# A hybrid encoder layer on one core: which early block stores the split weights, and where the last columns' raw weights are split

## The chip, the core and the metric

The kernel runs on one core of one Trainium2 chip. The metric is the device time of one execution in microseconds (us); smaller is better. The profile is of one other execution of the same program. Its engines are named PE (matmul) and PEld (its weight loads), DVE (VectorE), ACT (ScalarE), POOL (GpSimd) and SP (SyncE, which here only issues DMA).

## The reference

One layer of a streaming encoder over 2048 prompt rows, 16 meta rows and 64 sample rows of width 1024, all in float32. Cut to what matters here:

```python
def _trunk(x, states, segs, p):
    ...
        m, ns = _mixer(_rmsnorm(x, p['norm1_w'][l]), l, *st, segs, p)
        x = x + m
        x = x + _swiglu(_rmsnorm(x, p['norm2_w'][l]), p['w_gate'][l], p['w_up'][l], p['w_down'][l])
    ...
    return _rmsnorm(x, p['final_norm_w']), [jnp.stack(lst) for lst in new]

def _swiglu(h, wg, wu, wd):
    return (jax.nn.silu(h @ wg) * (h @ wu)) @ wd
```

`_mixer` is one input projection, three parallel groups of recurrent heads (SSD, RWKV-7, HGRN2) and one output projection of their 1536 outputs. `w_gate` and `w_up` are 1024 x 2816, `w_down` is 2816 x 1024. The outputs are the normed rows and the heads' states.

## The kernel before

**Numbers in two parts.** Each float32 matmul is made of three products of parts: a high part (`hi`, a copy on ACT into the float32r type) and a low part (`lo`, the difference from the raw number). `load_unit` (L191 to L206) brings one unit of weights, 128 x 512 numbers, into the ring: a tile `w` with both parts (512 KB, 5 buffers, WB) and, when the unit has not been split yet, a tile `raw` (256 KB, 3 buffers, RB). The first time, it loads `raw` (L200, on SP), copies to `hi` (L201, ACT), subtracts for `lo` (L203: three units of four on POOL, the fourth on DVE) and stores both parts in DRAM (L205, on SP); the dictionary `split` remembers where. Each later time it loads both parts in one DMA (L197).

**Stages.** The 17 row tiles are first projected in three double chunks (`projection`, from 0 to about 1350 us in the profile). Two streams of mixers are woven into everything up to about 2600 us: `flow` adds up the cost that each piece of the main stream yields and steps a mixer when its due time has come. The first nine tiles then go through `Ffn` in three early blocks of three tiles (320, 384 and 384 rows, `EARLY`); in order: the output projection `out`, with 24 units of `w_out`, and `ffn` over the 22 columns f of the hidden layer. For every f, `gemm_cm` (L238) takes two units of `w_gate` (k0 = 0 and k0 = 4) and two of `w_up`, with 12 matmuls each, and yields 12 x rows/2360 us of cost for each. Columns go in pairs (CF = 2); for a pair `down_units` loads four units of `w_down` (two columns by two halves of the output), and `down_tile` adds their products to `acc`, a yield of 3 x 2 x 512/2360 for each tile and half. That is 132 units for each block. So block 1 (`fs[0]`) splits and stores all of them, and blocks 2 and 3 load parts. For block 2 the pieces of the FFN yield 11 x (8 x 1.95 + 6 x 1.30) = 258 units of cost in all.

**Sums of quarters.** The last eight tiles take another path (`tokens_first` and `columns`) that needs sums of weight quarters. After the output projection of block 2, `prep_sums` is added as a stream: twelve groups, 35 cost units apart, of four raw loads (`t_sums`, L1367, on SP, into the same three `raw` buffers), four subtractions or additions on DVE (L1375 to L1383) and four stores (L1372, on POOL's queue).

**The end of block 3.** Block 3 runs `ffn(0, SWITCH)` with SWITCH = 18 beside the mixers. When these are done, the columns from 18 on and `rest` run as `last_early`, woven with `last_rows`, which loads the 24 pieces of mixer output that the last eight tiles need (`ya`, L1494), each with rows in pieces of 512 bytes; both take SP's queue.

**The last norm.** At the end of `tokens_first("wd", ...)`, `final_norm` (L1147) takes each of four chunks: squares of the second half on ACT (L1145; those of the first half were taken earlier, after product a12, in `rows_done`), their sum on DVE (L1154), the inverse root on POOL (L211), two multiplications of 128 x 512 on DVE (L1158), and two stores.

The order of each engine's instructions is set at build time by a scheduler with a timeline of its own. A piece may so be issued far ahead of its place in the program, as soon as a buffer is free; among pieces that want the same kind of buffer the program's order holds.

## Time and profile before

| what | us |
|---|---|
| three timed runs: median (lowest, highest) | 3490.52 (3483.44, 3492.62) |
| the profiled execution, its own time | 3493.2 |
| its span, first to last instruction | 3491.4 |
| early block 1, FFN (132 units) | 1452 to 1863 |
| early block 2, FFN | 1905 to 2310 |
| early block 3, FFN up to column 18 | 2352 to 2600 |
| early block 3, the last columns | 2600 to 2710 |
| the last eight tiles | 2710 to the end |

The page gives the span and the engines' busy time. Below them stands each resource in 40 slices of 87 us: the digit is its busy share in tenths, and the last row gives what the 16 DMA engines moved.

```profile
span 3491.4 us, 61048 instructions
...
DMA  8776875665776667999899897786778568875866
GB/s 312 230 235 213 291 229 169 178 176 162 230 236 190 195 191 263 313 321 317 310 315 320 314 330 245 241 270 217 230 244 260 199 206 276 299 266 169 292 191 215
```

The eight slices of 310 to 330 GB/s from the 17th on are blocks 1 and 2. In rows of the views by line, the form is: line, engine, operation, tiles written and read, shape, count, then busy time, mean ns of one, and idle time before it with what ended it. In rows of one line's instructions it is: count, shortest/median/longest ns, first and last start in us. A stage's row gives its length, each engine's busy time with its count of instructions, the granted PE clock, the busy share of the DMA engines, and GB/s.

### The profile page before, as it was taken

Reading aid. Unit: us, or ns where it says so; the run is one execution under the profiler, and the core shown is the slowest. Engines: PE = TensorE matmul, PEld = TensorE weight load, DVE = VectorE, ACT = ScalarE, POOL = GpSimd, SP = SyncE. Lnnn points to the kernel's source line nnn. Section 1 sums busy time; section 2 is a strip of 40 time slices with the busy share of each in tenths; the row PEclk is TensorE's granted clock in tenths of the full one; section 3 lists DMA queues with packets and bytes.
Section 4 is the critical chain, followed back from the end, with each engine's and each line's share of the span. In section 5 each row is a group of like instructions: output and inputs, shape, how many; then the busy total and the mean of one; then the engine's idle time right before and its main releaser. Section 6 shows DMA issues by size and latency. Waiting matters only on the chain.

```text
span 3491.4 us, 61048 instructions
## 1 busy us (share of the span) xinstructions
PE 3357.3 (96%) x22588; PEld 2936.8 (84%) x22588; DVE 2206.7 (63%) x4978; ACT 1238.9 (35%) x2678; POOL 783.0 (22%) x1122
## 2 busy tenths in 40 slices
PE   7999999999999999898998999999999999999998
PEld 7999689999789997787777888979888887888787
DVE  4268565477766676777877567676643675665453
ACT  4445333344443343453452212242211352233342
POOL 3324202102112112444442111011100123431001
PEclk9999999999999999999999999999999999999999
DMA  8776875665776667999899897786778568875866
GB/s 312 230 235 213 291 229 169 178 176 162 230 236 190 195 191 263 313 321 317 310 315 320 314 330 245 241 270 217 230 244 260 199 206 276 299 266 169 292 191 215
DMA packets 427123, 860.42 MB, mean 246 GB/s; under 512 B 112432, under 2 KB 212280, under 8 KB 424776
## 3 DMA queue, kind: packets, MB, share of 16 engines
q1 hardware_dynamic: 394376, 749.01, 65.5%
q0 software_dynamic: 32448, 107.50, 8.4%
q8 instruction: 178, 2.92, 0.3%
q14 instruction: 121, 0.99, 0.1%
HBM read 603.81 MB, written 252.54 MB: 245 GB/s over the span
## 4 chain that ended last, share of the span: by engine, by line
PE 69%; DMA 11%; DVE 10%; issue 4%; ACT 2%; POOL 2%; SPq 2%; POOLq 0%; DVEq 0%; ACTq 0%
PE g L109 47%; PE d L109 11%; PE c L109 5%; PE h L109 4%; DMA w<-w 3%; DMA raw<-in_w_up 1%; DMA raw<-in_w_out 1%; DVE gcv L407 1%; POOL w L203 1%; DVE Xp L630 1%; DVE tp L629 1%; PE po L109 1%; DMA hg<-stage 1%; DMA b4k<-psc 1%; DMA raw<-in_w_gate 1%
## 5 line engine op out<-in xcount | busy, mean ns | idle before, releaser
L109 PE MATMUL g<-hhi,w 128*128 128x384 f32 (+3 forms) x5424 | 1388.7, 333 | 27.8 <-DMA w<-w 10.8
L109 PEld LDWEIGHTS g<-hhi,w 128*128 128x128 f32 x5424 | 961.3, 190 | 53.4 <-DMA w<-w 10.4
L109 PE MATMUL g<-hlo,w 128*128 128x384 f32 (+3 forms) x2736 | 901.6, 330 | 1.3 <-DVE hlo L236 1.2
L109 PEld LDWEIGHTS g<-hlo,w 128*128 128x128 f32 x2736 | 516.4, 189 | 10.9 <-DVE hlo L236 2.2
L203 POOL TENSOR_TENSOR w<-raw,w 128x512 fp32r<-128x512 f32 x180 | 249.9, 1390 | 328.3 <-ACT w L201 262.8
L109 PE MATMUL g<-w,hhi 128*128 128x512 f32 (+1 forms) x832 | 273.3, 407 | 17.5 <-DMA w<-w 14.1
L109 PE MATMUL g<-w,mhi 128*128 128x512 f32 x792 | 263.3, 407 | 9.6 <-ACT w L201 3.8
L201 ACT ACTIVATE w<-raw 128x512 fp32r<-128x512 f32 x240 | 150.1, 627 | 178.0 <-PE g L109 51.5
L109 PEld LDWEIGHTS g<-w,hhi 128*128 128x128 f32 (+1 forms) x832 | 152.5, 189 | 55.4 <-DMA w<-w 16.6
L109 PEld LDWEIGHTS g<-w,mhi 128*128 128x128 f32 x792 | 146.6, 189 | 45.9 <-DVE acc L1323 6.5
L629 DVE TENSOR_TENSOR tp<-Xp,b4k 128x60 f32<-128x60 f32 (+24 forms) x527 | 122.0, 231 | 71.2 <-DMA b4k<-psc 58.4
L109 PE MATMUL g<-w,hlo 128*128 128x512 f32 (+1 forms) x416 | 165.9, 401 | 0.0
L109 PE MATMUL g<-w,mlo 128*128 128x512 f32 x396 | 158.0, 399 | 0.0
L1323 DVE TENSOR_TENSOR acc<-g,acc 128x512 f32<-128x512 f32 (+1 forms) x198 | 133.1, 682 | 34.1 <-PE g L109 34.0
L109 PE MATMUL g<-w,op 128*128 128x512 f32 x600 | 142.8, 396 | 0.0
L109 PEld LDWEIGHTS g<-w,op 128*128 128x128 f32 x600 | 112.6, 188 | 27.1
L630 DVE TENSOR_TENSOR Xp<-Xp,tp 128x60 f32<-128x60 f32 (+24 forms) x527 | 124.5, 236 | 13.1
L345 DVE SCALAR_TENSOR_TENSOR stage<-graw,cvec,stage 128x384 f32<-128x384 f32 (+2 forms) x98 | 55.1, 564 | 117.6 <-ACT graw L340 50.9
L109 PE MATMUL d<-ya,w 128*128 128x512 f32 x528 | 124.4, 392 | 0.7 <-DMA w<-w 0.7
L211 POOL TENSOR_TENSOR rs<-ss,half 128x1 f32<-128x1 f32 (+2 forms) x51 | 36.4, 719 | 378.7 <-DVE ss L209 236.2
L109 PEld LDWEIGHTS d<-ya,w 128*128 128x128 f32 x528 | 99.1, 188 | 22.8 <-DMA w<-w 1.1
L109 PE MATMUL d<-w,op 128*128 128x512 f32 x492 | 115.9, 396 | 0.0
(455 smaller groups left out, 5941.0 us busy)
## 6 DMA issues: line engine op xcount, KB each, us to landing
w<-w SPq DMA_DIRECT2D x893, 512.0 KB, 4.3
hin<-hg SPq DMA_DIRECT2D x16, 1280.0 KB, 7.1
rin<-rw SPq DMA_DIRECT2D x16, 896.0 KB, 5.7
raw<-in_w_gate SPq DMA_DIRECT2D x56, 256.0 KB, 4.6
raw<-in_w_up SPq DMA_DIRECT2D x56, 256.0 KB, 5.1
hg<-stage SPq DMA_DIRECT2D x64, 192.0 KB, 2.5
raw<-in_w_out SPq DMA_DIRECT2D x48, 256.0 KB, 5.3
sin<-ss SPq DMA_DIRECT2D x16, 768.0 KB, 4.9
```

What stands on the lines that cost most here:

```text
L109: return T.matmul(out, lhsT, rhs, start=start, stop=stop, skip_group_check=more)
L201: S.activation(hi, raw, AF.Copy)
L203: (G if units[0] % 4 < GLO else V).tensor_tensor(lo, raw, wt[:, 0], SUB)
L211: G.tensor_tensor(rs[:n], ss[:n], half[:n, 0:w], ALU.pow)
L345: V.scalar_tensor_tensor(st[:, a0:a1], raw[:, s0:s0 + a1 - a0], mu, st[:, a0:a1], MUL, ADD)
L407: V.scalar_tensor_tensor(cvt[:, :M], raw[:, j:j + M], tap(j), cvt[:, :M], MUL, ADD)
L629: V.tensor_tensor(tv, _bc(Xp[:, 0:m, q], 2, w), _bc(Up[:, q, q + 1:32], 1, m), MUL)
L630: V.tensor_tensor(Xp[:, 0:m, q + 1:32], Xp[:, 0:m, q + 1:32], tv, ADD)
L1323: V.tensor_tensor(self.acc[:n, i, cs], ps[:n], self.acc[:n, i, cs], ADD)
```

## The change

Four edits in one:

- `load_unit` takes `keep` and `again`. Without `keep`, a raw unit is split and not stored, so the next block that wants it loads it raw once more. With `again`, a unit is loaded raw and split although its parts are in DRAM.
- `Ffn.keep(k0)`: in block 1, only the units with k0 = 0 (for `w_down`, the first column of a pair) are stored. Block 2 loads the parts of these, and loads raw, splits and stores the others. `w_out` goes as before. `Ffn.again(f)`: in block 3, the 24 units of the columns from 18 on are loaded raw and split, and not stored.
- `last_rows` issues the 24 loads of `ya` from POOL's queue instead of SP's, ordered by row half, chunk and group rather than by group first, with one yield for each instead of two.
- `final_norm`, where the first half's squares were taken ahead (the last four chunks): that half is multiplied by the norm's weight on DVE right after its squares, in `rows_done`, and at the end by the inverse root alone, on ACT; the second half stays on DVE.

```diff
@@ -188,12 +188,13 @@
     units = [0]
     split = {}
 
-    def load_unit(src):
+    def load_unit(src, keep=True, again=False):
+
 
         key = str(src)
         wt = mk(ring, [P, 2, 512], F32, tag="w", bufs=WB)
         hi, lo = wt[:, 0].bitcast(F32R), wt[:, 1].bitcast(F32R)
-        if key in split:
+        if key in split and not again:
             nc.sync.dma_start(wt, split[key])
             return hi, lo
         raw = mk(ring, [P, 512], tag="raw", bufs=RB)
@@ -201,6 +202,8 @@
         S.activation(hi, raw, AF.Copy)
         units[0] += 1
         (G if units[0] % 4 < GLO else V).tensor_tensor(lo, raw, wt[:, 0], SUB)
+        if again or not keep:
+            return hi, lo
         d = split[key] = dram.tile([P, 2, 512], F32, tag=f"w{units[0]}", name=f"w{units[0]}")
         nc.sync.dma_start(d, wt)
         return hi, lo
@@ -235,11 +238,11 @@
         S.activation(ho, pt[:, :, :n], AF.Copy)
         V.tensor_tensor(lw, pt[:, :, :n], ho.bitcast(F32), SUB)
 
-    def gemm_cm(w, hTs):
+    def gemm_cm(w, hTs, keep=lambda k0: True, again=False):
 
         banks = [gbank() for _ in hTs]
         for k0 in range(0, KD, 4):
-            hi, lo = load_unit(w[:, k0 * P:(k0 + 4) * P])
+            hi, lo = load_unit(w[:, k0 * P:(k0 + 4) * P], keep(k0), again)
             for ps, ((hhi, hlo), n) in zip(banks, hTs):
                 for k in range(k0, k0 + 4):
                     wh, wl = (x[:, (k - k0) * P:(k - k0 + 1) * P] for x in (hi, lo))
@@ -1146,6 +1149,8 @@
 
     def final_norm(p, xt, t, n, fw, queue, s2=None):
 
+
+        weighted = s2 is not None
         ss = mk(p, [P, 1], tag="ss", bufs=2)
         if s2 is None:
             s2 = mk(p, [P, 2], tag="s2", bufs=2)
@@ -1155,7 +1160,10 @@
         rs = inv_rms(p, ss, n, 1, 1.0 / D, EPS)
         for hf in range(2):
             cs = slice(hf * 512, hf * 512 + 512)
-            V.scalar_tensor_tensor(xt[:, cs], xt[:, cs], rs[:n], fw[:n, cs], MUL, MUL)
+            if weighted and hf == 0:
+                S.activation(xt[:, cs], xt[:, cs], AF.Copy, scale=rs[:n])
+            else:
+                V.scalar_tensor_tensor(xt[:, cs], xt[:, cs], rs[:n], fw[:n, cs], MUL, MUL)
             queue.dma_start(O["y_prompt"][(t - 1) * P:t * P, cs] if t else O["y_sample"][:, cs], xt[:, cs])
 
     class Ffn:
@@ -1278,8 +1286,8 @@
             for f0 in range(fa, fb, CF):
                 mhi, mlo = self.hl(self.fp, "m", CF, 2)
                 for f in range(f0, f0 + CF):
-                    pg, = yield from gemm_cm(A["w_gate"][f], [(self.hT, self.N)])
-                    pu, = yield from gemm_cm(A["w_up"][f], [(self.hT, self.N)])
+                    pg, = yield from gemm_cm(A["w_gate"][f], [(self.hT, self.N)], self.keep, self.again(f))
+                    pu, = yield from gemm_cm(A["w_up"][f], [(self.hT, self.N)], self.keep, self.again(f))
                     sg = self.w2k()
                     h_, l_ = mhi[:, f - f0, NS], mlo[:, f - f0, NS]
                     S.activation(sg[:, NS], pg[:, NS], AF.Tanh, scale=0.5)
@@ -1310,7 +1318,16 @@
                     yield 3 * CF * 512 * COL
 
         def down_units(self, f0, hf):
-            return [load_unit(A["w_down"][f * P:(f + 1) * P, hf * 512:hf * 512 + 512]) for f in range(f0, f0 + CF)]
+            return [load_unit(A["w_down"][f * P:(f + 1) * P, hf * 512:hf * 512 + 512], self.keep(4 * (f - f0)), self.again(f))
+                    for f in range(f0, f0 + CF)]
+
+        def keep(self, k0):
+
+            return k0 == 0 or self is not fs[0]
+
+        def again(self, f):
+
+            return self is fs[-1] and f >= SWITCH
 
         def down_tile(self, i, hf, mhi, mlo, wds):
             o, n, cs = self.offs[i], self.lens[i], slice(hf * 512, hf * 512 + 512)
@@ -1488,11 +1505,10 @@
     ya = {m: mk(lqa, [P, 2, 4, 512], F32, tag="ya", bufs=3) for m in (2, 0, 1)}
 
     def last_rows():
-        for m in (2, 0, 1):
-            for h in range(2):
-                for j in range(NH):
-                    nc.sync.dma_start(ya[m][:, h, :, j * P:j * P + P], yscr[m][tile_of(h, j)])
-                    yield 0.0
+        for h in range(2):
+            for j in range(NH):
+                for m in (2, 0, 1):
+                    G.dma_start(ya[m][:, h, :, j * P:j * P + P], yscr[m][tile_of(h, j)])
                     yield 0.0
 
     def last_early():
@@ -1733,6 +1749,7 @@
                 final_norm(l2, acc[1][j], tile_of(1, j), P, fw, G)
             elif a == "a12":
                 squares(l2, acc[0][j], P, 0, sq[j])
+                V.tensor_tensor(acc[0][j][:, :512], acc[0][j][:, :512], fw[:, :512], MUL)
 
     acc = [[mk(l2, [P, D], tag=f"acc{h}{j}", bufs=1) for j in range(NH)] for h in range(2)]
     fw = mk(l2, [P, D], tag="nw", bufs=1)
```

## The prediction

> **What bounds the kernel now.** I began with the page: which engine is busy, and how large a load of weights is.
>
> ```profile
> PE 3357.3 (96%) x22588; PEld 2936.8 (84%) x22588; DVE 2206.7 (63%) x4978; ACT 1238.9 (35%) x2678; POOL 783.0 (22%) x1122
> ...
> w<-w SPq DMA_DIRECT2D x893, 512.0 KB, 4.3
> ```
>
> PE is busy 96% of the span, so only a stage in which PE lacks something can give time back. PE's busy time hides short gaps, because matmuls overlap; weight loads (PEld) show them better. So next I read the busy time by stage: the projection, the FFN of early block 1, that of block 2, the FFN of block 3 while the mixers run, and its end in two pieces.
>
> ```profile
> core 0: us, PE busy (x) PEld busy (x) DVE busy (x) ACT busy (x) POOL busy (x), PEclk, DMA share, GB/s
> 60.00:350.00 290.00, 284.59 (x1931) 272.88 (x1929) 155.46 (x366) 133.56 (x288) 105.25 (x168) 0.99 0.72 231
> ...
> 1452.00:1863.00 411.00, 383.49 (x3003) 331.14 (x3003) 321.49 (x669) 173.86 (x376) 180.84 (x148) 0.97 0.91 318
> ...
> 1905.00:2310.00 405.00, 396.34 (x2904) 350.94 (x2906) 275.59 (x663) 105.84 (x253) 67.81 (x89) 0.99 0.82 280
> ...
> 2352.00:2600.00 248.00, 243.70 (x1888) 222.48 (x1886) 146.37 (x357) 53.84 (x131) 25.22 (x27) 0.99 0.71 226
> 2600.00:2640.00 40.00, 29.57 (x121) 26.43 (x120) 19.85 (x23) 6.15 (x8) 0.00 (x0) 0.83 1.04 315
> 2640.00:2710.00 70.00, 70.00 (x353) 63.21 (x352) 25.47 (x43) 8.00 (x19) 1.16 (x3) 1.00 0.71 234
> ```
>
> PEld's share is 331.14/411 = 0.81 in block 1, 350.94/405 = 0.87 in block 2, 222.48/248 = 0.90 in block 3, and 0.66 against 0.90 in the last two rows. So block 1 and the 40 us at 2600 are the loose places. Block 1 is also where DMA is busiest over a long time (0.91 of the engines, 318 GB/s), since it reads raw weights and writes both parts back. What ends last there is seen in the chain of work within that window, and in its raw loads (L200), copies (L201) and subtractions (L203):
>
> ```profile
> by line: PE g L109 30.3%; DMA raw<-in_w_up 8.1%; PE c L109 5.9%; issue 5.3%; POOL w L203 5.1%; DMA raw<-in_w_down 5.0%; PE h L109 3.7%; DMA raw<-in_w_gate 3.4%; DMA hin<-hg 1.9%; DVE acc L1323 1.8%; DMA w<-w 1.7%; ACT w L201 1.6%; DVE Xp L6
> ```
> ```profile
> DMA to landing us min/median/max: 3.2/4.7/9.3
> ```
> ```profile
> L201 ACT ACTIVATE w<-raw x127: 612/631/682, 1459.0 to 1821.2; 128x512 fp32r<-128x512 f32 x127
> ```
> ```profile
> L203 POOL TENSOR_TENSOR w<-raw,w x96: 1262/1298/2667, 1452.0 to 1823.6; 128x512 fp32r<-128x512 f32 x96
> ...
> L203 DVE TENSOR_TENSOR w<-raw,w x33: 655/684/1698, 1451.6 to 1820.7; 128x512 fp32r<-128x512 f32 x33
> ```
>
> The second of these fences is the landing of the raw loads (min, median, max). Block 1's FFN has 132 units (22 columns f with 4 gate and up units and 2 down units each). The copies of 127 of them lie 362.2/126 = 2.87 us apart. With three raw buffers one trip of a buffer takes 3 x 2.87 = 8.6 us: 4.7 landing, 0.63 copy, 1.14 subtraction (three of four on POOL), and 2.1 of issue and waits. So block 1 runs partly at the pace of the raw ring, and loads are 8.1 + 5.0 + 3.4 = 16.5% of its chain, 68 us.
>
> **Part 1: fewer stores in block 1.** Units with k0 = 4 and the second down unit of each pair are no longer stored: 66 of 132, 66 x 0.524 = 34.6 MB and 66 issues on SP fewer. Block 1 now moves 411 us x 318 GB/s = 131 MB; 96 MB remain, 251 GB/s at 383 us. The projection, at 231 GB/s, shows what a raw load (L200) takes when DMA has room:
>
> ```profile
> DMA to landing us min/median/max: 3.2/3.8/5.0
> ```
>
> By line between 3.8 at 231 and 4.7 at 318 GB/s, loads land in 4.0, which is 0.7 sooner; a trip takes 7.9 us, a unit 2.64, and 132 units gain 30 us. Two bounds: if only loads on the chain count, 68 x 0.7/4.7 = 10 us; if PEld's share rises to block 3's, 411 - 331.14/0.897 = 42 us. Block 2's share, the nearest row (same loops and mixers), gives 411 - 331.14/0.867 = 29. I take **-28**. Late next is DVE: its 321 us would fill 84% of 383.
>
> **Part 2: block 2 splits and stores the other half.** Added are 66 copies of 0.63 us on ACT (42 us), about 50 subtractions of 1.30 on POOL (65) and 16 of 0.68 on DVE (11), and 66 stores; 66 loads of parts become raw ones of half the size. ACT, POOL and DVE have room (105.8, 67.8 and 275.6 busy of 405). Stores bring 34.6 MB and the halved loads take 17.3 away: 280 + 17.3 MB/405 us = 323 GB/s, about block 1's load now. Two things do not hide so surely.
>
> The first is the raw ring. In block 2 the sums of weight quarters use it alone today, twelve groups of four loads (L1367) and four stores (L1372). The first fence has the stores, with their landing, the second the loads of parts, the third a wait of SP (total, times, longest):
>
> ```profile
> L1372 POOLq EVENT_SEMAPHORE x44: 17/17/17, 1874.4 to 2107.5; - x44
> ...
> DMA to landing us min/median/max: 2.6/5.3/8.1
> ```
> ```profile
> L197 SPq DMA_DIRECT2D w<-w x140: 319/320/1586, 1920.1 to 2305.6; - x140
> ```
> ```profile
> SPq L1367 <- DMA wo2t<-raw: 11.0, 4, 4.2
> ```
>
> A group takes 4 x 233.1/43 = 22 us. After the change each stands between raw units in the order of the program, every 35 cost units; block 2's FFN has 258 of them, so 7 groups fall among its units. The raw unit behind a group gets its buffer only when the group's second sum is stored: a load of 4.7, a subtraction 0.7, a store 5.3, then its own load 4.7 and split 0.63 + 1.30: 17.3 us after the split of the raw unit ahead of the group. Without the group it would be split two units later, 2 x 2.77 = 5.5 (385.5 us/139 loads). Of the 11.8 us of delay, the five w buffers cover 4 x 2.77 - 1.93 = 9.1. Left are 2.7 a group, 19 us in all. Bounds: 0, because no PE wait of block 2 comes near the 11.0 us that SP waits for wo2's stores today, and 7 x (22 - 9.1) = 90 if nothing of a group overlaps raw units. The nearest row, SP's wait, is hidden entirely, but beside loads of parts alone; I take half of 19, +10.
>
> The second is DVE beside a busy POOL: the same instruction (L821, two inputs in SBUF) in block 1 and in block 2, the mean in ns behind the busy time.
>
> ```profile
> L821 DVE TENSOR_TENSOR hin<-hin,tot 128x256 f32<-128x256 f32 x18 | 14.0, 779 | 0.0
> ```
> ```profile
> L821 DVE TENSOR_TENSOR hin<-hin,tot 128x256 f32<-128x256 f32 x15 | 6.3, 418 | 0.0
> ```
>
> It takes 1.86 times as long where POOL is busy 181 of 411 us. POOL will be busy 65 us more in block 2; with DVE at 0.54 of its speed then, and busy 68% of the time, it loses at most 65 x 0.46 x 0.68 = 20 us, out of 130 idle. 0 to 20; I take +3. The Trainium skill, in the page "GPSIMD Engine Reference", section "Key points", says that GpSimd shares its SBUF interfaces with VectorE and contends with instructions that have two SBUF inputs. By that rule the trace agrees, 779 against 418 ns, and the full effect is the first rival below, against this part.
>
> Block 2: **+13**, 0 to 90.
>
> **Part 3: last columns and the mixer rows.** At 2600 SP issues 24 loads of ya (L1494), with few loads of weights between them, and PE waits for w:
>
> ```profile
> 2603.86 6.53 SPq L1494 DMA_DIRECT2D ya<-y  x6
> ...
> 2624.46 4.71 SPq L1494 DMA_DIRECT2D ya<-y  x4
> 2629.27 85.02 SPq L197 DMA_DIRECT2D w<-w  x40
> ```
> ```profile
> PE g L109 <- DMA w<-w: 8.3, 4, 4.2
> ```
> ```profile
> L863 POOL DMA_DIRECT2D out_p_hgrn<-Shg x1: 816/816/816, 2589.2 to 2589.2; - x1
> ```
>
> An issue of ya takes SP 1.1 us (6.53/6). At a share of 0.90 the window's 26.43 us of weight loads need 29.3, so 40 - 29.3 = 11 us are lost. After the change SP is free for 24 raw loads, half as large, and POOL issues the rows: 24 x 0.82 (L863, the nearest form, also pieces of 512 bytes) = 20 us, plus 18 subtractions of 1.30, 23: 43 us of POOL within PE's 24 x 2.13 = 51 us (85.02/40). ACT (15 us of copies) and DVE (4) have room in the last window row. A raw unit comes every 2.64 us, as in part 1: 24 x 0.51 = 12 us too slow, less the 9.1 that the ring holds ready. Bounds: -11, and +7 where subtractions also stand behind some five row issues on POOL (3 + 4). I take **-7**.
>
> **Part 4: the tail.** The last chunk's norm (L1154) waits for both multiplications (L1158) of the chunk before:
>
> ```profile
> 3481.91 1.41 DVE L1158 SCALAR_TENSOR_TENSOR acc<-acc,rs,nw 128x512 f32<-128x512 f32 x2 [0.73 <-POOL rs L211]
> 3483.24 0.15 DVE L1154 TENSOR_TENSOR ss<-sq 128x1 f32<-128x1 f32 x1
> ...
> 3484.31 1.42 DVE L1158 SCALAR_TENSOR_TENSOR acc<-acc,rs,nw 128x512 f32<-128x512 f32 x2 [0.73 <-POOL rs L211]
> ```
>
> With one of each pair on ACT, L1154 comes 0.7 earlier and the last pair is 0.7 shorter: **-1.4** (0 if the output's DMA sets the end). The four new products on DVE fall in the down stage, under PE's matmuls.
>
> **Sum.** -28 + 13 - 7 - 1.4 = -23.4. The profiled execution took 3493.2 us, 2.7 over the median shown (3490.52); 3493.2 - 23.4 = 3470. A measurement of this kernel can tell about 0.3% (10.5 us) from no change.
>
> **Rivals.**
>
> *Block 2 becomes what block 1 was* (0.22). For it: the same DMA load (323 GB/s), L821, and DVE at 276 + 11 + 20 = 307 of 405, 76%, near block 1's 78%. At block 1's share of 0.806 it takes 350.94/0.806 = 435, +30: 3493.2 - 28 + 30 - 8.4 = 3487. Against it: only half of the units go through the raw ring.
>
> *Block 1 is not held by its loads* (0.14). DVE and the mixers hold it, and only the 10 us come: 3493.2 - 10 + 13 - 8.4 = 3488. For it: DVE at 78%, and only 16.5% of the chain is loads. Against it: block 2 has a share of 0.87 beside the same mixers.
>
> *The sums hold the raw ring* (0.12), slower. If a group's 22 us overlap no raw unit, each costs 12.9 us, 7 of them 90: 3493.2 - 28 + 90 - 8.4 = 3547; halfway, 3502. It decides from (28 + 8.4)/7 = 5.2 us a group on. For it: three buffers in strict order. Against it: that same order gives the 2.7 above.
>
> **Chances.** The forecast, 3440 to 3483, has 0.52. Faster by over 0.3%: that and a quarter of the first rival, 0.58. Within 0.3%: the rest of the first and most of the second, 0.28. Slower: the third and a little of the others, 0.14. The range goes down to 42 us in part 1 with 0 in part 2, -11 in part 3 and -1.4 (3439), and up past 3487 and 3488 to the third's halfway, 3502.
>
> **What would show it.** Step 1: raw loads in block 1 land in about 4.0, units come 2.64 us apart, and the window's PEld share is 0.86 or more. Step 2: block 2's FFN lasts some 418 us, the sums' stores are spread over it and on into block 3, L821 takes about 600 ns there, and PE waits behind a group for w from ACT or POOL by 1 to 3 us. Step 3: near 2600 PE has no wait for w over 2 us, SP issues raw loads steadily, and POOL the rows at about 0.8 each. Step 4: one L1158 for each of the last chunks on DVE, an ACT copy beside it. I am wrong if block 1 keeps its 2.87 us a unit, or if block 2's FFN takes over 440 us.

## The result, and the profile after

The changed kernel takes 3523.72 us (median; 3516.78 to 3525.14) against 3489.73 us before, measured together on one chip: a ratio of 1.0091, with a 95% interval of 1.0070 to 1.0112. It is slower by about 34 us, where the forecast had 3470 us. The profiled execution took 3522.48 us, 29.3 us over that of before. Two executions among the experiments below ran at a granted clock of 0.234 and 0.707, where all others have 0.98 to 0.99, and no median or stage time here uses them. The page after:

```profile
span 3520.4 us, 61352 instructions
...
PE 3367.2 (96%) x22588; PEld 2943.8 (84%) x22588; DVE 2257.2 (64%) x5000; ACT 1294.7 (37%) x2772; POOL 894.4 (25%) x1214
...
DMA  9776875565776667767687778897766567884766
GB/s 316 234 222 214 298 230 168 169 180 162 233 232 182 198 198 281 268 223 242 220 300 258 267 266 274 309 347 251 226 215 217 190 204 269 296 285 162 292 197 215
...
w<-w SPq DMA_DIRECT2D x803, 512.0 KB, 4.5
```

The change did what it says: 90 loads of parts fewer, and the eight slices from the 17th on carry 220 to 300 GB/s instead of 310 to 330. (These slices end at about 2095 us, so they are block 1 and the first half of block 2; the three behind them carry more than before, 274, 309 and 347 against 245, 241 and 270.) PE has the same 22588 matmuls to do. The busy time by stage shows where the time went; the columns are those of the rows quoted in the prediction, and the windows are moved with the stages.

```profile
core 0: us, PE busy (x) PEld busy (x) DVE busy (x) ACT busy (x) POOL busy (x), PEclk, DMA share, GB/s
...
1452.00:1838.00 386.00, 365.17 (x2913) 319.42 (x2912) 317.32 (x641) 170.20 (x369) 179.61 (x144) 0.99 0.73 241
...
1880.00:2336.00 456.00, 421.80 (x3006) 370.76 (x3007) 324.40 (x738) 148.69 (x330) 131.97 (x133) 0.95 0.82 279
```

Block 1 is 25 us shorter, with a PEld share of 319.42/386 = 0.83 (0.81 before). Block 2 is 51 us longer, with 370.76/456 = 0.81 (0.87 before), and its DMA engines are no busier than before, 0.82. To follow one place through all kernels I use five marks: the first matmul of the first block's out-projection (on y3hi), the first tanh of each early block (ACT, w2k from g), and the first down product d of the last eight tiles. These are two such marks, block 3's first tanh before and after, from the view by line:

```profile
L1285 ACT ACTIVATE w2k<-g x2: 487/488/490, 2369.8 to 2377.5; 128x384 f32<-128x384 f32 x2
```
```profile
L1293 ACT ACTIVATE w2k<-g x1: 494/494/494, 2395.7 to 2395.7; 128x384 f32<-128x384 f32 x1
```

| stage, us | before | after | difference |
|---|---|---|---|
| start to the first out-projection | 1356.5 | 1357.6 | +1.1 |
| to the first tanh of block 1 | 102.1 | 100.4 | -1.7 |
| B1: to the first tanh of block 2 | 466.1 | 440.6 | -25.5 |
| B2: to the first tanh of block 3 | 445.1 | 497.1 | +52.0 |
| B3: to the first d | 355.9 | 362.3 | +6.4 |
| to the end | 765.7 | 762.4 | -3.3 |

So block 1 gained nearly what was forecast, and B2 took back twice that. But B1, B2 and B3 do not hold the same work before and after, because the mixers are woven in by due time. The rows of B1, before and after (those of B2 stand in the next section), show it in PE's count:

```profile
1458.60:1924.70 466.10, 431.19 (x3319) 369.52 (x3317) 362.82 (x792) 194.29 (x431) 191.17 (x164) 0.97 0.91 316
```
```profile
1458.00:1898.60 440.60, 414.99 (x3186) 359.93 (x3179) 359.29 (x753) 188.69 (x410) 188.24 (x154) 0.98 0.74 246
```

B1 lost 133 matmuls, B2 gained 31 and B3 101 (2280 to 2381). The whole stretch from the first out-projection to the first d, called E below, holds 9291 matmuls before and 9290 after; it went from 1369.2 to 1400.4 us, +31.2. In B2, PE is without a matmul for 9.9 us before (445.1 - 435.2) and 37.6 after (497.1 - 459.5). That is 27.7 of the 52.0 us. The other 24.3 are longer busy time of PE, for 31 more matmuls and at a granted clock of 0.95 instead of 0.99. Whether the lower clock comes of the waits was not tried.

In B2, this is what SP's queue waits for, before (first fence) and after (second):

```profile
SPq L197 <- PE g L109: 204.0, 110, 6.2
```
```profile
SPq L198 <- PE g L109: 95.7, 51, 5.0
SPq L208 <- POOL w L204: 66.2, 32, 9.6
...
SPq L1384 <- DMA wo0t<-raw: 9.2, 1, 9.2
...
SPq L201 <- DMA wo2t<-raw: 8.3, 3, 4.4
```

Before, SP was so far ahead that for 204 of 445 us it waited only for PE to give a w buffer back. After, this is 95.7 of 497; instead it stands at the stores of parts (L208, for POOL's subtraction), at the sums' loads (L1384) and at raw loads whose buffer a sum's store still reads (L201). The timeline shows SP standing at a sum's load, with a raw piece of w_gate behind it in line; 9.2 us of this is the wait for the store of wo0t in the rows above. ACT then waits for late raw pieces:

```profile
1992.66 10.29 SPq L1384 DMA_DIRECT2D raw<-in_w_out  x2
2003.06 0.37 SPq L201 DMA_DIRECT2D raw<-in_w_gate  x1
```
```profile
ACT w L202 <- DMA raw<-in_w_gate: 41.8, 8, 12.7
```

### The profile page after: what moved, and what is told of

It is laid out like the page before. It is cut to its first block, busy times and chain, and to the rows that moved or that the text cites. A ratio compares the mean times of both kernels' runs of the same rounds, so it can differ in the third digit from the quotient of the medians.

```text
span 3520.4 us, 61352 instructions
## 1 busy us (share of the span) xinstructions
PE 3367.2 (96%) x22588; PEld 2943.8 (84%) x22588; DVE 2257.2 (64%) x5000; ACT 1294.7 (37%) x2772; POOL 894.4 (25%) x1214
## 5 line engine op out<-in xcount | busy, mean ns | idle before, releaser
L109 PEld LDWEIGHTS g<-hhi,w 128*128 128x128 f32 x5424 | 960.3, 189 | 56.3 <-DMA w<-w 11.8
L204 POOL TENSOR_TENSOR w<-raw,w 128x512 fp32r<-128x512 f32 x248 | 346.3, 1401 | 506.0 <-ACT w L202 459.7
L202 ACT ACTIVATE w<-raw 128x512 fp32r<-128x512 f32 x330 | 206.6, 629 | 335.6 <-PE g L109 153.6
L632 DVE TENSOR_TENSOR tp<-Xp,b4k 128x60 f32<-128x60 f32 (+24 forms) x527 | 134.2, 255 | 69.7 <-DMA b4k<-psc 56.8
L1340 DVE TENSOR_TENSOR acc<-g,acc 128x512 f32<-128x512 f32 (+1 forms) x198 | 133.6, 683 | 35.1 <-PE g L109 34.6
L109 PEld LDWEIGHTS d<-w,op 128*128 128x128 f32 x492 | 92.5, 188 | 22.3
```

Of the source, the lines that this page charges most:

```text
L109: return T.matmul(out, lhsT, rhs, start=start, stop=stop, skip_group_check=more)
L202: S.activation(hi, raw, AF.Copy)
L204: (G if units[0] % 4 < GLO else V).tensor_tensor(lo, raw, wt[:, 0], SUB)
L632: V.tensor_tensor(tv, _bc(Xp[:, 0:m, q], 2, w), _bc(Up[:, q, q + 1:32], 1, m), MUL)
L1340: V.tensor_tensor(self.acc[:n, i, cs], ps[:n], self.acc[:n, i, cs], ADD)
```

## The experiments

Three theories were tried for B2. **R**: the sums and the raw pieces, which split the same three raw buffers, wait for each other's buffers. **S**: SP's in-order queue, held by sums or stores, brings everything behind it late. **A**: ACT's in-order queue stands at the late copy. A fourth, **V**, is VectorE's part in the sums. The times of B1, B2, B3 and E of all kernels stand in a table at the end of this section; each is read from one profiled execution, and the timed runs of one kernel lie up to some 15 us apart, so a few us between two rows decide nothing. Code cuts are against the changed kernel, except where the kernel before is named; `...` marks lines left out.

**Which part, and are the sums it?** The first kernel has only `keep`, without the three other edits (`again` off, rows and norm as before). The second leaves the first twelve groups of sums out of the changed kernel, the third leaves them out of the kernel before.

```diff
-            return self is fs[-1] and f >= SWITCH
+            return False
...
```


> The first part of the change alone: half of the units stored in block 1, the other half in block 2; mixer rows, last columns and last norm as before the change. All theories: block 1 about 26 us shorter, block 2 about 48 us longer as in the changed kernel. From column 16 on the two profiles differ by 6 us (the changed kernel is slower there) and at the tail by 1.5 the other way, so about 3518; if the last columns were not the cause of those 6 us, 3524.

Measured: 3520.47 us (median of three runs), ratio 1.0079 (1.0053 to 1.0105). `keep` alone makes the loss, as far as three runs can tell; the other parts cancel to within the measurement. This kernel has no row in the table of stages.

```diff
             for kk in kks:
-                t_sums(f"{key}{kk}", quarters(key, kk), nc.sync)
+                q = quarters(key, kk)
+                for s, n in (("t3", 3), ("t1", 1), ("t2", 0), ("t4", 2)):
+                    d = tdram[f"{key}{kk}", s] = dram.tile([P, 512], F32, ...)
+                    G.dma_start(d, q[n])
                 yield 35.0
```


> The changed kernel, but the sums of weight quarters are left out: in their place the 48 quarters are copied from DRAM to DRAM at the same points of the program, so no raw buffer, no DVE addition and no SP issue is used for them, while their DMA bytes stay. Block 2 is read from its first to its last FFN tanh, 332 us before the change and 379 after it. Theory A (the sums and block 2's raw units hold each other up in the ring of three raw buffers): block 2 falls to 330 to 345 us and the kernel to about 3480. Theory B (block 2 is now what block 1 was: DMA load, a busy POOL slowing DVE): block 2 stays at 365 or more and the kernel over 3510. Theory C (SP's queue stands at the sums' loads and the parts behind it come late): as A here.

> The kernel before with the first twelve groups' sums left out and copies from DRAM to DRAM in their place, as was done to the changed kernel (it leaves out those additions and subtractions). From the first block's out-projection to the third block's first tanh the kernel before takes 1013 us, the changed kernel 1038, the changed kernel without sums 995. If the sums cost next to nothing beside parts, as the forecast had it: 1005 to 1013 us here, the halved stores are worth 10 to 18 us, and the kernel takes 3482 to 3490. If they cost about as much there as beside raw pieces: 985 us or less, the halved stores are worth nothing, and the kernel takes 3462 or less. Between, in proportion.

The copies of both kernels have nothing to wait for and ran in the first microseconds, where they delay the first out-projection by 25.3 and 31.7 us (last section), so the whole times, 3500.7 and 3516.75 us, say nothing of the sums. B2 does. In order: before, before without sums, after, after without sums.

```profile
1924.70:2369.80 445.10, 435.22 (x3212) 383.11 (x3212) 304.43 (x752) 114.44 (x274) 67.87 (x88) 0.99 0.82 279
```
```profile
1956.50:2401.10 444.60, 440.12 (x3288) 389.80 (x3287) 292.44 (x749) 116.51 (x276) 48.27 (x55) 0.99 0.72 237
```
```profile
1898.60:2395.70 497.10, 459.49 (x3243) 401.45 (x3242) 348.54 (x801) 158.27 (x358) 138.85 (x143) 0.95 0.84 286
```
```profile
1926.20:2377.90 451.70, 443.49 (x3350) 389.51 (x3350) 317.56 (x743) 159.09 (x360) 116.59 (x104) 0.99 0.81 273
```

In B2 the sums cost 0.5 us beside parts (445.1 - 444.6) and 45.4 beside raw pieces (497.1 - 451.7). Splitting and storing half of block 2 costs 7.1 us by itself (451.7 - 444.6). Over E, where all four kernels have the same matmuls, the sums cost 7.0 us beside parts (1369.2 - 1362.2) and 50.5 beside raw pieces (1400.4 - 1349.9), and without them the change gains 12.3 (1362.2 - 1349.9). The copies took the sums' bytes out of block 2 as well, so this shows that the sums make the loss, and not yet by which resource.

**Which resource?** One edit of the changed kernel at a time: the sums' loads on POOL's queue; the copy of block 2's raw pieces on POOL; the stores of their parts on POOL's queue; five raw buffers and four w.

```diff
-                t_sums(f"{key}{kk}", quarters(key, kk), nc.sync)
+                t_sums(f"{key}{kk}", quarters(key, kk), G)
```


> The changed kernel with the sums' raw loads issued from POOL's queue instead of SP's; the buffers stay shared. C: SP never stands at a sum, block 2 falls to about 340 us and the kernel to 3485. A: the ring still orders them, block 2 stays at 365 or more, the kernel at 3510 to 3525. B: no difference, 3515 to 3525.


```diff
-        S.activation(hi, raw, AF.Copy)
+        if here:
+            G.tensor_copy(hi, raw)
+        else:
+            S.activation(hi, raw, AF.Copy)
```


> The changed kernel, with one edit: the raw pieces that the second block loads are copied into the high half by POOL, not by ACT; nothing else moves. Theory A (ACT's queue stands at the copy of a raw piece that came late because the sums hold the three raw buffers, and everything behind it on ACT, the tanh, the mixers' copies and evictions, waits too): without that copy on ACT the second block falls from 379 us tanh to tanh to 355 or less, ACT's idle time ended by the raw loads (41.8 and 16.1 us in the changed kernel) goes, and the kernel takes 3496 to 3504. Theory B (it does not matter which engine splits; the late pieces themselves reach TensorE, or POOL and SP stand in ACT's place): 372 us or more, 3514 to 3526. Between 355 and 372 both have a part.


```diff
-        nc.sync.dma_start(d, wt)
+        (G if here else nc.sync).dma_start(d, wt)
```


> The changed kernel, with one edit: in the second block the parts of a split piece are stored by POOL's queue and not by SP's. In the changed kernel SP's queue stands 60.5 us of that block's 379 at these stores (they follow the loads in SP's order and wait for POOL's subtraction), 14.2 us more for VectorE's, and it is ahead of TensorE for 43 us alone (150.6 us in the kernel before). Theory S (SP's in-order queue, held by the stores and the sums' loads together, has lost its run-ahead, and every load behind it, the parts and the mixers' inputs, comes late): without the stores on SP the second block falls from 379 us to 358 or less and the kernel takes 3496 to 3506. Theory R (the three raw buffers alone are what stands; whichever queue issues, the group and the raw piece wait for each other's buffers): the second block stays at 370 us or more and the kernel at 3514 to 3526.


```diff
-RB, WB = 3, 5
+RB, WB = 5, 4
```


> The changed kernel with five raw buffers and four pairs of parts in place of three and five; the bytes are the same. Theory A (the raw ring is what the second block lacks): the second block falls from 379 us to 355 or less, while the first block and the stretches that only load parts may lose by the fifth pair that is gone (unknown, 0 to 40 us in the whole). Theory B (ring depth is not it): the second block stays at 372 us or more.

The first two took 3519.02 and 3529.04 us, with B2 at 510.2 and 515.1: no gain. Theory A fell: where ACT does not stand, something else does. The first also says that SP's standing at the sums' loads alone is not the cause. The third took 3511.7 us at a ratio of 1.0066 (1.0045 to 1.0087), with block 2 at 366 us from first to last tanh (379 before that edit), but B2 at 495.3: most of what was gained came back as loss in the next out-projection, and SP stood at raw loads instead (L204 for POOL and DVE, 29.7 and 24.9 us). Relieving SP of one kind of wait is not enough. The fourth decides nothing: block 2 fell to 357, the out-projection after it grew from 118 to 146, and 3527.0 us came of it; a pair of parts was given up for the raw buffers.

**Buffers of their own.** SBUF is full there, so a control came first: 6 KB of each partition taken from the mixers' 4 KB buffers and the block's row buffer. Then these 6 KB go to the sums as three buffers.

```diff
-    b4k = lambda: mk(mx, [P, 1024], tag="b4k", bufs=3)
+    b4k = lambda: mk(mx, [P, 1024], tag="b4k", bufs=2)
...
-                yr = yr or mk(yp[0], [P, 4, P], tag="yr", bufs=2)
+                yr = yr or mk(yp[0], [P, 4, P], tag="yr", bufs=1)
```


> The changed kernel with 6 KB a partition taken from other buffers (two, not three, of the mixers' 4 KB buffers, one, not two, for the mixer rows of a block). It is the control for the next run: every theory expects it as slow as the changed kernel or slower, 3524 to 3580, with 497 us or more from the first tanh of the second block to the first of the third.


```diff
-            r = mk(ring, [P, 512], tag="raw", bufs=RB)
+            own = queue is nc.sync
+            r = mk(fe[0] if own else ring, [P, 512], tag="traw" if own else "raw", bufs=3 if own else RB)
```


> The control, with the 6 KB given to the sums as three buffers of their own, in the second block, on SP's queue as before; the raw pieces have the three raw buffers to themselves. Theory R (sums and raw pieces wait for each other's raw buffers): from first tanh to first tanh of the two blocks 25 to 45 us less than the control, and the kernel 25 to 45 us less. Theory S (SP's queue stands at the sums' loads, whatever buffers they have) and theory V (VectorE's share): less than 12 us from the control.

The control took 3521.29 us with B2 at 496.0. With own buffers the kernel took 3510.46 and B2 458.2, as R had it, but the reading is not clean: nothing held the sums back any more, and their loads moved into block 1 (1386.5 to 1681.7 us), whose B1 and out-projection grew by 22.5 us over the control's (454.8 + 118.2 against 438.9 + 111.6). So I held them, by an order on SP's queue behind block 2's residual loads:

```diff
-            queue.dma_start(r, q[n])
+            in_turn(([after_] if own else []) + [queue.dma_start(r, q[n])])
```


> The control with 6 KB taken from other buffers, these given to the sums as three buffers of their own, and the sums' loads held on SP's queue behind the second block's residual loads, so that they run in the second block and later as in the control. Theory R (sums and raw pieces wait for each other's raw buffers): from the second block's first tanh to the third's 465 us or less (control 496), and the kernel 3484 to 3498. Theory S (SP's queue stands at the sums' loads whatever buffers they have, and VectorE's part on top): 485 us or more, and 3510 to 3526. Between, both have a part.

> The same kernel as the one with the sums held in the second block with three buffers of their own. Theory R: from the second block's first tanh to the third's 465 us or less (control 496), SP's waits for the sums' stores ahead of raw pieces gone; theory S: 485 us or more.

It took 3495.32 us, ratio 1.0015 (1.0002 to 1.0029), 26 us less than the control. The same kernel again took 3493.57, ratio 1.0019 (1.0005 to 1.0033), 28 less, and B2 is, for the control and for it:

```profile
1907.20:2403.20 496.00, 461.04 (x3381) 401.71 (x3380) 358.27 (x830) 163.37 (x370) 144.27 (x150) 0.96 0.85 292
```
```profile
1906.70:2367.50 460.80, 443.53 (x3248) 393.18 (x3247) 344.68 (x795) 158.72 (x358) 135.56 (x135) 0.98 0.88 304
```

B2 is 35.2 us shorter when the sums have three buffers of their own, on the same queue, with the same loads and operations, and PE is without a matmul for 17.3 us instead of 35.0. Not all of the 35.2 is gain: B2 holds 133 matmuls fewer, and B3 got longer (359.3 against 348.6). The hold also spread the sums: of their 48 loads 11 come before B2, 32 in it and 5 after it, in the control 4, 44 and 0. Over E, with 9276 matmuls against 9275, the control takes 1395.0 us and this kernel 1368.0: 27.0 less, as in the whole times. So theory R holds for about half of the 50.5 us, the largest part that one edit took back with the sums kept in block 2. Whether three more shared buffers would do the same is not settled, since the run with five raw buffers gave up a w. What is left was not separated between S and V. VectorE's operations were left out by themselves:

```diff
-        V.tensor_tensor(a, a, b, SUB)
...
-        V.tensor_tensor(b, b, c_, SUB)
...
```


> The changed kernel with the sums' loads and stores in place, but without their four operations on VectorE a group: the pieces are stored as they were loaded (it leaves out the first twelve groups' additions and subtractions). Theory V (a group holds its buffers, and SP's queue, until VectorE comes to it, behind the mixers' and the block's work): 20 us or more less than the changed kernel from first tanh to first tanh (497 us), and in the whole. Theory R and S hold with or without them, since load and store alone take the buffers 5 to 15 us: less than 12 us gained.

Without VectorE's operations, on the shared buffers: 3507.55 us, B2 at 478.9, 18 less than 497.1 (E 14.3 less), between what the two theories expected. A group without them also holds its buffers for a shorter time, so this does not speak against R, and the part of VectorE's time cannot be told from that of the hold.

**Moving the sums away.** Into block 3, where no raw piece is read before column 18; first in the shared buffers, then (`again` off) in six of their own, taken when the early blocks' row buffers are given back; then with their loads on POOL's queue; and, from the second of these, with the parts of blocks 1 and 2 stored by POOL.

```diff
-            yield from f.out()
-            if i == 1:
+            if i == 2:
                 streams.append(Stream(prep_sums(), 1.0))
+            yield from f.out()
...
-                yield 35.0
+                yield 15.0
```


> The changed kernel with the groups of sums started at block 3 instead of block 2, 15 cost units apart instead of 35, nothing left out. A and C: block 2 at 330 to 345 us, block 3 unchanged to column 18 (it loads parts only), a kernel of about 3480, or some 10 us more if the last groups reach the raw units of the last columns. B: block 2 at 365 or more, about 3515.


```diff
...
                 stY.close()
+                yp.append(pool(stS, "sm", side="right", reuse_waits="tile"))
+                streams.append(Stream(prep_sums(), 1.0))
                 yield from f.ffn(0, SWITCH)
...
-            r = mk(ring, [P, 512], tag="raw", bufs=RB)
+            own = queue is nc.sync
+            r = mk(yp[1] if own else ring, [P, 512], tag="traw" if own else "raw", bufs=6 if own else RB)
...
```


> The changed kernel without the second reading of raw weights in the last columns, and with the sums begun after the out-projection of the third block, in six buffers of their own, so that they hold no raw buffer of the weights; groups 17 units of cost apart. If the raw buffers are what the sums and the raw loads fight for: second block 350 us or less tanh to tanh, third block to column 16 within 6 us of the kernel before (285 us from its first tanh to column 18), and the kernel takes 3470 to 3482, faster than the kernel before. Rival: the sums cost what they cost wherever they stand, by SP's, DVE's and the DMA engines' time and not by the buffers: the third block is 12 us longer, as it was with the sums in the shared buffers there, and the kernel takes 3486 to 3494.

> The kernel with the sums in six buffers of their own in the third block (3486.47 us), with the sums' loads on POOL's queue and not on SP's. If SP's standing at them is what is left of their cost: from the third block's first tanh to column 16 254 us or less (260 there, 251 in the kernel before), and the kernel 3476 to 3482. If it is VectorE's share, the DMA engines' or the mixers' work that comes later: 258 us or more, 3484 to 3492.

> The kernel with the sums in six buffers of their own in the third block (no second reading of raw weights), and the parts of the first and the second block stored by POOL's queue and not by SP's. Theory S: SP's run-ahead grows in both blocks, their stalls (50 us in the first block, 37 in the second) fall by 10 to 30 us together, and the kernel takes 3458 to 3478. Theory R, or POOL made the bound by the issues (some 170 in the first block, some 75 in the second, under 1 us each, beside a POOL that is busy half of the first block): no gain or a loss, 3482 to 3500.

3495.33 us (ratio 1.0010, 0.9996 to 1.0024), 3486.47 (0.9996, 0.9984 to 1.0009), 3482.15 (0.9979, 0.9966 to 0.9991) and 3523.55 (1.0104, 1.0077 to 1.0131). The third is faster than both kernels, by 0.2% over the kernel before; the intervals of the second and the third overlap. Own buffers in block 3 do not make the sums free: from its first tanh to column 16 it takes 260.4 us and 257.5 with POOL's queue, 250.8 before. Whether SP's queue makes any of these 10 us is not resolved: a difference of 3 us is no more than the spread of executions, and the two profiled ones took 3480.36 and 3486.97 us, the other way round than the medians. The last one failed on the side of its rival: B1 is 20 us longer than with the stores on SP (459.5 against 439.1). What of POOL's work makes that was not separated.

**The last columns.** The kernel before with `again` alone, then with `again` and the rows on POOL:

```diff
...
-            return k0 == 0 or self is not fs[0]
+            return True
...
```


> The kernel before with one part of the change alone: in the last columns of the third block the weights are read raw and split again; the first block stores all parts, rows and norm are the old ones. If the last columns lose by it: from column 18 to the first down product of the last block's tail 4 to 10 us longer than before, and the kernel 3494 to 3500. If the forecast's third part was right and only the rest of the change hid it: 3480 to 3488. Rival: no difference, 3488 to 3493.

> The kernel before with two parts of the change: the last columns of the third block read raw weights again, and the last block's mixer rows are loaded by POOL's queue in the new order. The second reading alone changed nothing in the last columns (from column 18 to the first down product 71 us, as before), the changed kernel took 79. If POOL's queue, standing at the rows' loads ahead of its subtractions for the raw pieces, makes the 8 us: 78 us or more here, and 3496 to 3502. If the 8 us come from what the first and second block leave behind (late sums, late stores): 72 us or less, and 3486 to 3492.

3493.61 us (1.0005, 0.9992 to 1.0017) and 3485.73 (0.9995, 0.9982 to 1.0008): neither differs from before. From column 18 on they take 71.1 and 77.3 us to the first d, before it was 71.0. So the first does not lose there, and the second comes near the 78 expected if POOL's queue costs something, but its whole time is not the 3496 to 3502 that went with it. The stage from column 16 to the first d does, a little. In order: before, after, `again` alone, `again` with rows:

```profile
2620.60:2725.70 105.10, 100.49 (x482) 90.01 (x481) 45.59 (x69) 15.60 (x31) 10.15 (x18) 0.96 0.81 273
```
```profile
2648.90:2758.00 109.10, 100.35 (x480) 87.73 (x481) 57.89 (x80) 33.41 (x58) 42.87 (x46) 0.98 0.67 221
```
```profile
2618.70:2722.70 104.00, 99.26 (x481) 88.46 (x481) 53.09 (x75) 30.25 (x55) 33.31 (x36) 0.98 0.63 216
```
```profile
2612.30:2720.70 108.40, 100.26 (x480) 87.71 (x481) 61.20 (x80) 33.27 (x58) 42.48 (x47) 0.98 0.65 223
```

Both together cost 3 to 4 us here. In the twelve kernels of this document that have both edits the stage takes 102.2 to 111.6 us, the middle one 108, and in the six others of the table 103.5 to 105.1, so the cost is likely but not there in each. A reason that fits is that the same POOL queue issues the rows and subtracts for the raw pieces. In these four rows POOL is busy 43 against 33 us, and in the changed kernel it waits 10.1 us for earlier rows to land before it issues the next. PE shows no wait for POOL's subtraction in this stage, so the reason is not shown. The changed kernel's waits of POOL:

```profile
POOL w L204 <- ACT w L202: 38.4, 12, 13.1
POOL ya L1511 <- DMA ya<-y: 10.1, 10, 2.3
```

All stages, from the same marks. The medians were taken on several chips; the kernel before took 3485.26 to 3490.68 us beside them.

| kernel | median us | B1 | B2 | B3 | E |
|---|---|---|---|---|---|
| before | 3489.73 | 466.1 | 445.1 | 355.9 | 1369.2 |
| after | 3523.72 | 440.6 | 497.1 | 362.3 | 1400.4 |
| before, no sums | 3516.75 | 467.2 | 444.6 | 349.3 | 1362.2 |
| after, no sums | 3500.70 | 443.1 | 451.7 | 354.9 | 1349.9 |
| sums' loads on POOL | 3519.02 | 444.9 | 510.2 | 348.6 | 1405.5 |
| copy on POOL | 3529.04 | 447.2 | 515.1 | 352.5 | 1415.3 |
| part stores on POOL | 3511.70 | 438.7 | 495.3 | 351.5 | 1387.5 |
| five raw, four w | 3527.00 | 441.6 | 502.4 | 357.6 | 1388.9 |
| control, less 6 KB | 3521.29 | 438.9 | 496.0 | 348.6 | 1395.0 |
| own buffers | 3510.46 | 454.8 | 458.2 | 350.1 | 1381.3 |
| own buffers, held (run again) | 3493.57 | 443.7 | 460.8 | 359.3 | 1368.0 |
| no operations of the sums | 3507.55 | 444.7 | 478.9 | 360.7 | 1386.1 |
| sums in block 3, shared | 3495.33 | 441.4 | 466.2 | 365.8 | 1373.6 |
| sums in block 3, own | 3486.47 | 439.1 | 458.0 | 363.9 | 1362.2 |
| the same, POOL's queue | 3482.15 | 445.2 | 459.1 | 361.5 | 1368.3 |
| own, part stores on POOL | 3523.55 | 459.5 | 471.6 | 363.3 | 1396.3 |
| `again` alone | 3493.61 | 469.8 | 442.6 | 355.4 | 1369.7 |
| `again`, rows on POOL | 3485.73 | 466.1 | 442.1 | 353.2 | 1363.3 |

## Why the prediction was wrong

**Part 1 came out by its number, in part by luck**: -28 forecast, -25.5 measured over B1, and -24.1 between the two kernels without sums (467.2 to 443.1). Raw loads land sooner, as forecast (4.0; the second row is of the copies that follow them):

```profile
DMA to landing us min/median/max: 2.4/3.8/8.7
```
```profile
L202 ACT ACTIVATE w<-raw x127: 613/632/686, 1456.6 to 1804.1; 128x512 fp32r<-128x512 f32 x127
```

The copies lie 347.5/126 = 2.76 us apart, from 2.87, where I had 2.64; and PEld's share rose to 0.83 only, not 0.86. Most of the gain in B1 is mixers' work that slid into later stages: of the 25.5 us, 16.2 are busy time of PE (431.19 to 414.99, with 133 matmuls fewer), and only 9.3 are time in which PE has no matmul (34.9 to 25.6). That is the lower bound of the working, 10 us, and what the rival that block 1 is not held by its loads had; this rival is not out. Over E without the sums the change gains 12.3 us, where the forecast without its term for the sums had -28 + 3 - 7 = -32.

**Part 2 is the step that failed**: +13 forecast, +52.0 measured over B2. DVE beside a busy POOL is not what made it: what I had priced at +3 is part of the 7.1 us that B2 loses without sums, and the instruction that I had put at about 600 ns in block 2 took

```profile
L824 DVE TENSOR_TENSOR hin<-hin,tot 128x256 f32<-128x256 f32 x17 | 9.3, 548 | 0.0
```

as a mean. This mean hides two groups: 15 of the 17 took 406 to 423 ns, as in block 2 before, and two took 1526 and 1530. In block 1 before, likewise, 12 of 18 took 408 to 420 ns and six 1504 to 1521. So the instruction is not slower all the time, as my factor of 0.54 had it; now and then it takes 1.1 us more. By the rule of the Trainium skill that I weighed there ("GPSIMD Engine Reference", section "Key points": GpSimd contends with VectorE instructions that have two SBUF inputs) the trace agrees, 548 against 418 ns, but as the main effect, my first rival, it fails: B2 without sums has the same splitting and takes 451.7 us.

The term that was mis-sized is that of the raw ring and the sums: +10 forecast; the sums cost 45.4 us in B2, and over E 50.5 where they cost 7.0 before, 43.5 more. The number of groups was about right. I counted 7 among block 2's FFN units; of the sums' 48 loads 4 run in block 1 (1798.0 to 1812.6 us), 25 between block 2's first and last tanh, 16 in the out-projection behind it, and 3 in block 3's FFN. The 25 loads, some six groups, cost 379.4 - 344.3 = 35.1 us, 5.6 a group, where I had 2.7 and took half. The 16 in the out-projection, which the sum had at nothing, cost 10.3 (117.7 - 107.4). So it is the price that failed: I let five w buffers cover 9.1 us of the 11.8 that a group delays the raw piece behind it, and halved the rest. That cover is SP's lead over PE, and the lead shrank: the time in which SP waited for PE alone fell from 204.0 of 445 us to 95.7 of 497, and SP stood at the stores of split pieces instead. Half of the loads of block 2 still had full pairs of parts, but in order behind the raw ones. That the lost lead is what makes a group dear is argued, not shown: without the sums SP waits for PE for 137.6 of 451.7 us, so the splitting takes the larger part of the lead by itself, and B2 loses only 7.1 us by it. A delay can also pass to everything in line behind, ACT's copies and the mixers' loads. PE itself shows few waits for a late split,

```profile
PE g L109 <- ACT w L202: 7.2, 4, 3.6
```

about as long as the 1 to 3 us each that I had forecast; the rest is spread over the mixers' matmuls and others. And the row that I took as the nearest, SP's 11.0 us for wo2's stores, was hidden because those sums had the raw buffers nearly to themselves (B2 is 0.5 us shorter without them). It could say nothing of what a raw piece behind them would cost.

The rival "the sums hold the raw ring", with 0.12, is what came nearest, at half of its full price: its halfway case of 3502 had 45 us for the sums. What lies between 3502 and 3522 is mostly part 3 and the split itself. No term of the sum had the clock, which fell from 0.99 to 0.95 in B2.

**Part 3 had the wrong sign**: -7 forecast; the stage from column 16 to the first d went from 105.1 to 109.1 us, +4.0. PE's long waits for w at 2600 did go, and the rows were issued at the price forecast,

```profile
L1511 POOL DMA_DIRECT2D ya<-y x24: 747/747/768, 2633.6 to 2665.6; - x24
```

but with the rows on POOL and parts still loaded, that stage is 103.5, 104.0 and 104.8 us in the three kernels with own buffers in block 3, so the rows on SP cost 0.3 to 1.6 us and not 11. PEld's share of 0.90 that I set as the target was not reached there: 86.17/103.5 is 0.83. My upper bound, +7 by subtractions behind row issues on POOL, fits what came, and as said above it is not shown. The remaining 2.4 us of B3 lie before column 16, where the last three of the sums' loads run (to 2408.5 us) and B3 holds 101 matmuls more; they were not separated.

**Part 4 came as forecast in this pair**: -1.4 forecast; from the last matmul to the end the kernel before takes 11.0 us and the changed one 9.5. Over all profiles here this stretch is 9.7 to 11.0 us with the old norm and 7.9 to 12.9 with the new one, so a gain of 1.5 us is not settled by it. One multiplication of each pair is on ACT now, beside the other on DVE:

```profile
3514.31 0.75 DVE L1166 SCALAR_TENSOR_TENSOR acc<-acc,rs,nw 128x512 f32<-128x512 f32 x1 [0.73 <-POOL rs L214]
```
```profile
3514.31 0.72 ACT L1164 ACTIVATE acc<-acc,rs 128x512 f32<-128x512 f32 x1 [1.11 <-POOL rs L214]
```

By the steps as they came: -25.5 + 52.0 + 6.4, and -3.9 in the other rows of the stage table, is +29.0, the difference of the two spans.

## What to carry to other kernels

A ring of buffers that one stream has to itself looks free, because its long waits hide; a second stream put on it pays for a part of each hold, here 5.6 us of some 22 a group. Bound the price of such a meeting by the hold (load, operation, store) times the number of visits, and do not credit the lead of the queue that feeds it as a cover without looking at what the change does to that lead. Compare stages only over stretches that hold the same work: here the count of matmuls showed that most of a stage's gain had moved elsewhere. Where the second stream can be held to another stage, or be given buffers of its own, the change's gain stays: here the sums in block 3, with their own buffers and POOL's queue, and `again` off, turned +34 us into -6.

## What the runs showed of the hardware

Copies from DRAM to DRAM that depend on nothing were issued in the first 64 us and were not free. In the kernel before without sums, POOL is busy 39.84 us of the first 60, and PE gets 15.36 us of work done where it got 39.44 (first fence: before; second: without sums), which the rest of the kernel did not make up: the first out-projection starts at 1388.2 us, not 1356.5.

```profile
0.00:60.00 60.00, 39.44 (x200) 36.14 (x201) 30.32 (x65) 26.30 (x64) 20.29 (x52) 0.94 0.93 323
```
```profile
0.00:60.00 60.00, 15.36 (x83) 13.80 (x83) 15.97 (x45) 17.28 (x39) 39.84 (x81) 1.00 0.95 340
```

The 24 loads of mixer rows took a median of 0.71 us each to issue on SP (0.52 to 2.55) and 0.75 on POOL (0.75 to 0.77), so by the median neither queue is the cheaper; the 1.1 us of the working were the mean of six issues in one row of the timeline. On POOL, waits of 14.9 us in all for earlier rows to land came on top.
